# A second norm that carries its weights by rows, and weight parts at two places modulo 256 bytes

## The chip, the cores and the metric

One core of one Trainium2 chip. The metric is the device time of one execution in microseconds (us), the median of several. The engines are TensorE (PE; its weight loads are shown apart as PEld), VectorE (DVE), ScalarE (ACT), GpSimd (POOL) and SyncE (SP), which issues most of the DMAs. TensorE's products land in PSUM, which has eight banks of 128 x 512 float32; everything else that the engines work on lies in SBUF.

## The reference

One layer of an encoder, for 512 rows of 1024 features in float32. What matters here is the second half:

```python
def layer(x):
    h = rmsnorm(x, g_pre_mix)
    q, k, v, g, u, sv, a_ret, a_sgu = split(h @ w_in)          # 1024 x 7168
    merged = sigmoid(a_ret) * retention(q, k, v, g) @ w_ret_o + sigmoid(a_sgu) * sgu(u, sv) @ w_sgu_o
    x1 = x + rmsnorm(merged @ w_out, g_post_mix)
    h2 = rmsnorm(x1, g_pre_ffn)
    hid = conv3(h2 @ w_up)                                     # 1024 x 5632, three taps along the rows, and a bias
    a, b = split(hid)
    return x1 + rmsnorm((gelu(a) * b) @ w_down, g_post_ffn)    # 2816 x 1024

def rmsnorm(x, g):
    return x * rsqrt(mean(x * x) + 1e-6) * g
```

## The kernel before

Each float32 operand of a product is split into a high part, which ScalarE copies (line 79 in `copy`), and a low part, which VectorE gets by subtraction (line 86 in `split`). A product is then three: high by high, high by low and low by high (`mm3`, lines 217 to 219). Of `w_up`, the weights are the stationary operand and the activations the moving one, so the result has features by partitions and rows along the free dimension. `w_down` and `w_out` go the other way round.

Many products come in couples of seven instead of eight (Strassen's scheme in Winograd's form): class `Pair`, whose products all stand on line 670. For these the weights are added in seven forms (`w_form`: B11, B21, T1, T2, T3, T4, B22; T2 and T4 on GpSimd, lines 170 and 172) and the activations in four sums S1 to S4 (`x_forms`). A product of a couple takes 256 of the 512 rows at a time ("in halves"); `T0` and `T1` are the two halves.

The stages, in the order of time: q and k (to 50 us); the retention part with v, the two halves of the SGU's second input and the gate g (to 216 us); `u` in couples (to 260 us); the gates `a_ret` and `a_sgu` in couples, each beside whole blocks of `w_ret_o` or `w_sgu_o` with 512 columns (to 426 us); `w_out` with the two norms (to 487 us); `w_up` (to 712 us); `w_down` (to 825 us); the last norm's rest.

The part around the change, in the kernel's words:

- `norms(t, acc)` does the two norms of one row block of 128 rows: the mean square on ScalarE (`mean_square`), the root on GpSimd (`row_scale`, whose result is called `qr`), `z` and the sum x1 on VectorE, then x1 times the scale of the second norm, called `xn` (line 871).
- `turn(t, zs)` lets TensorE transpose `xn` (line 882). ScalarE copies each block of 128 features from PSUM with its weight of `g_pre_ffn` as the scale into `h2h[k]` (line 886), VectorE makes `h2l[k]` of it (line 889). A weight stands by partition here, since features lie along the partitions.
- `early(e, q)` runs the first four blocks of `w_up` by halves of the rows, so that TensorE can begin with the rows whose norms are done.
- `f_block` runs one further block of `w_up`: 8 feature blocks by 3, in halves where `two` is set and over 512 columns otherwise. Blocks 4 to 7 (tiles 2 and 3) and the whole blocks of the gates take 512 columns.
- `h2_forms(k)`, called after tiles 0 and 1, adds `h2h` and `h2l` of two feature blocks on GpSimd (line 981, the sum is called `h`) and makes S1 to S4 of it (lines 300 to 303 and 79, 86). The couples of `w_up` (tiles 4 to 19) need them.
- `conv`, `gated` and `down_forms` turn the results of `w_up` into what `w_down` takes.

Tiles named `blk` are 512 columns wide and lie in a ring of 76; a weight part is a `slot` of 1088 columns, of which it uses 1024 from column `at` on. As built, every `blk` and every slot begins 64 bytes past a multiple of 256, so `at` (in columns of 4 bytes) sets a weight part's place modulo 256 bytes: 0 leaves it at 64, 16 puts it at 128, 32 at 192 and 48 at 0.

The order of the instructions on each engine is written by a scheduler that reads the program; the DMA queues keep that order too.

Of the kernel before, what the change touches and what calls it, by code (L numbers as in the profile page):

```python
# [10 lines left out]
F32 = mybir.dt.float32  # L11
# [29 lines left out]
PRE, FFNG, LNG, LNB = 0, 8, 16, 24  # L41
CW, CB = 32, 32 + 3 * 2 * NF
# [5 lines left out]
def tile_block(ctx: ExitStack, tc, xT, x, wall, par, cs, wsp, bsp, gpost, gffn, out):  # L48
# [77 lines left out]
    def halved(e):  # L126

        return e < EARLY or e >= 2 * COUPLES[0][0]

    def w_block(i):  # L130
# [26 lines left out]
    def w_form(form, i):  # L157
# [15 lines left out]
        w = slot("wf", 16)  # L173
        split(w[:, :S], w[:, S:], w_raw[form])
        return w[:, :S], w[:, S:]

    def w_down(form, i):
# [15 lines left out]
        hi, lo = slot("dh", 48, w), slot("dl", 48, w)  # L193
# [8 lines left out]

    def w_get(look=LOOK):
# [5 lines left out]
        while w_pos[1] < len(units) and (w_pos[1] <= i or n + w_size(units[w_pos[1]]) <= max(room, 9 if look == LOOK else 0)):  # L209
            u = units[w_pos[1]]  # L210
            w_ready[w_pos[1]] = w_unit(u)
            w_pos[1] += 1
            n += w_size(u)
# [8 lines left out]
    part = const("part", [P, NPAR + 8])[:, :NPAR]  # L222
# [418 lines left out]
    def f_block(ah, al, n, between=None, two=False):  # L641
# [3 lines left out]
        f = (T0, T1) if two else (slice(0, S),)  # L645
        for i in range(n * len(f)):
            if between and i == n * len(f) // 2:
                between()
            k, t = i % n, f[i // n]
            c = slice(k * P, (k + 1) * P)  # L650
            mm3(o[:, t], wh[:, c], wl[:, c], ah[k][:, t], al[k][:, t], k == 0, k == n - 1)
        return o

    class Pair:
# [3 lines left out]
        def __init__(self, func, alloc, a=None, scale=None):  # L658
            self.func, self.t, self.scale = func, [alloc(), alloc()], scale
            self.h, self.l, self.forms = a or (xh, xl, forms)  # L660
# [15 lines left out]
        def x(self, first, t):  # L676
            return lambda k: (self.h[first + k][:, t], self.l[first + k][:, t])
# [46 lines left out]
    for j in range(KD // 2):  # L724
        p = Pair(AF.Gelu_apprx_tanh, lambda: blk(n="u"), None, rbc)
# [40 lines left out]
    def gated_pair(ah, al, late=None):  # L766
        p = Pair(AF.Sigmoid, lambda: tmp("sig"), None, rbc)
# [77 lines left out]
    for k in range(KD):  # L845
        h2h.append(blk(F32R, "h2h"))
        h2l.append(blk(F32R, "h2l"))

    def norms(t, acc):
# [19 lines left out]
        for n in range(2):  # L869
            z = tmp("xn")  # L870
            v.tensor_scalar(
# [384 lines left out]
```

## Time and profile before

| | |
|---|---|
| median of three runs | 837.9 us (836.99 to 840.36) |
| the profiled execution | 835.91 us |
| its span, first to last instruction | 834.1 us |
| granted TensorE clock, mean | 0.993 |
| instructions | 14181 |
| TensorE products | 5632, busy 815.7 us |
| DMA | 93.31 MB, mean 112 GB/s |

The profile is of one execution. Its rows name an engine, a line of the kernel, an operation and its tiles (out<-in, buffer numbers left out), the shape, the count, and what ended the idle time before it. A product's end is modelled, and its recorded time (0.28 us for 256 columns, 0.39 us for 512) overlaps that of the next: how fast products follow each other is read from their starts or from their number in a stretch.

### The profile page before, as it was taken

To read this page: it belongs to the slowest core of one execution; us is meant where nothing else is said; L and a number is where in the kernel's file an instruction comes from. 1 tells how busy PE (TensorE), PEld (TensorE's weight loads), DVE (VectorE), ACT (ScalarE), POOL (GpSimd) and SP (SyncE) were. 2 spreads that over 40 slices of the span, in tenths; PEclk is the share of its full clock that TensorE was granted. 3 is DMA by queue.
4 is the path that set the end of the run, shared out by engine and by line. 5 is a ranking of instruction groups with operands and counts; after the bars stand their busy time and mean duration, and the time that the engine had idled before them with its cause. 6 is when DMAs were issued, how large, how long until landed. Compare 5 with 4: busy or idle time off the path is not lost.

```text
span 834.1 us, 14181 instructions
## 1 busy us (share of the span) xinstructions
PE 815.7 (98%) x5632; PEld 753.4 (90%) x5632; DVE 665.1 (80%) x1100; ACT 429.8 (52%) x729; POOL 110.4 (13%) x110
## 2 busy tenths in 40 slices
PE   9999999999999999999999999899999999999995
PEld 7888888888899999999988898799999999999995
DVE  7489888877897776867664769779899899997956
ACT  6635446545664533444444564456566565654531
POOL 0010000112221111132211225110211100000001
PEclk9999999999999999999999999999999999999998
DMA  8733222213233333323457120333333341243334
GB/s 290 244 114 106 74 74 77 75 51 102 86 104 103 102 102 101 102 76 111 140 157 301 60 68 26 102 101 102 102 103 101 101 153 51 77 127 108 120 127 152
DMA packets 29219, 93.31 MB, mean 112 GB/s; under 512 B 3360, under 2 KB 4000, under 8 KB 29152
## 3 DMA queue, kind: packets, MB, share of 16 engines
q1 hardware_dynamic: 26928, 86.85, 32.4%
q0 software_dynamic: 1360, 4.46, 1.6%
q10 hardware_dynamic: 864, 1.09, 0.4%
q8 instruction: 44, 0.72, 0.3%
q14 instruction: 23, 0.19, 0.1%
HBM read 88.19 MB, written 4.19 MB: 111 GB/s over the span
## 4 chain that ended last, share of the span: by engine, by line
PE 77%; DVE 15%; issue 3%; DMA 2%; ACT 1%; POOL 1%; DVEq 0%; POOLq 0%; ACTq 0%; SPq 0%
PE ps L670 18%; PE ps L217 10%; PE ps L218 10%; PE ps L219 10%; PE ps L1024 7%; PE ps L480 5%; PE ps L479 5%; PE ps L481 5%; DVE wf L86 2%; DVE wl L86 2%; DVE cv L931 2%; PE ps L820 2%; PE ps L819 2%; PE ps L818 2%; DVE cv L935 2%
## 5 line engine op out<-in xcount | busy, mean ns | idle before, releaser
L86 DVE TENSOR_TENSOR wl<-raw,wh 128x1024 fp32r<-128x1024 f32 (+1 forms) x93 | 110.7, 1199 | 49.3 <-PE ps L670 23.5
L79 ACT ACTIVATE wf<-raw 128x512 fp32r<-128x512 f32 x140 | 85.0, 627 | 100.8 <-PE ps L218 35.6
L86 DVE TENSOR_TENSOR wf<-raw,wf 128x512 fp32r<-128x512 f32 x140 | 106.4, 775 | 26.6 <-ACT wf L79 26.0
L670 PE MATMUL ps<-sh,wf 128*128 128x256 f32 x640 | 121.7, 280 | 2.2 <-ACT sh L79 1.7
L217 PE MATMUL ps<-h2h,wh 128*128 128x256 f32 (+1 forms) x416 | 118.7, 287 | 0.0
L219 PE MATMUL ps<-h2h,wl 128*128 128x256 f32 (+1 forms) x416 | 118.6, 286 | 0.0
L218 PE MATMUL ps<-h2l,wh 128*128 128x256 f32 (+1 forms) x416 | 118.6, 286 | 0.0
L79 ACT ACTIVATE wh<-raw 128x1024 fp32r<-128x1024 f32 (+2 forms) x95 | 93.2, 990 | 35.3 <-DMA raw<-wall 14.7
L670 PEld LDWEIGHTS ps<-sh,wf 128*128 128x128 f32 x640 | 102.0, 189 | 3.4 <-ACT sh L79 1.9
L670 PE MATMUL ps<-sl,wf 128*128 128x256 f32 x320 | 89.6, 280 | 1.5 <-DVE sl L86 1.5
L217 PEld LDWEIGHTS ps<-h2h,wh 128*128 128x128 f32 x416 | 78.3, 189 | 1.5 <-ACT h2h L886 0.3
L218 PEld LDWEIGHTS ps<-h2l,wh 128*128 128x128 f32 x416 | 78.3, 188 | 1.3
L219 PEld LDWEIGHTS ps<-h2h,wl 128*128 128x128 f32 x416 | 78.3, 188 | 1.2
L479 PE MATMUL ps<-wh,xh 128*128 128x512 f32 x192 | 75.0, 391 | 0.0
L480 PE MATMUL ps<-wl,xh 128*128 128x512 f32 x192 | 74.9, 390 | 0.0
L481 PE MATMUL ps<-wh,xl 128*128 128x512 f32 x192 | 74.8, 390 | 0.0
L170 POOL TENSOR_TENSOR raw<-raw,raw 128x512 f32<-128x512 f32 x20 | 34.4, 1718 | 218.5 <-DVE raw L168 184.4
L670 PEld LDWEIGHTS ps<-sl,wf 128*128 128x128 f32 x320 | 61.1, 191 | 2.0 <-DVE sl L86 1.7
L1024 PE MATMUL ps<-dl,fh 128*128 128x256 f32 x216 | 59.9, 278 | 1.5 <-DVE dl L86 1.5
L1024 PE MATMUL ps<-dh,fh 128*128 128x256 f32 x216 | 60.0, 278 | 1.2 <-DVE e L1058 1.0
L1024 PE MATMUL ps<-dh,fl 128*128 128x256 f32 x216 | 59.8, 277 | 0.0
L670 PE MATMUL ps<-xh,wf 128*128 128x256 f32 x288 | 54.5, 281 | 0.0
(303 smaller groups left out, 2051.5 us busy)
## 6 DMA issues: line engine op xcount, KB each, us to landing
raw<-wall SPq DMA_DIRECT2D x145, 512.0 KB, 3.6
x<-x SPq DMA_DIRECT2D x24, 256.0 KB, 6.1
xT<-xT SPq DMA_DIRECT2D x8, 256.0 KB, 5.5
x<-x POOLq DMA_DIRECT2D x8, 256.0 KB, 2.3
xT<-xT POOLq DMA_DIRECT2D x4, 256.0 KB, 3.9
out<-zg SPq DMA_DIRECT2D x4, 256.0 KB, 2.2
out<-zs ACTq DMA_DIRECT2D x3, 256.0 KB, 3.7
cs<-cs SPq DMA_DIRECT2D x2, 256.0 KB, 4.2
```

Source lines behind the costliest of these rows:

```text
L79: nc.scalar.activation(out=o, in_=i, func=AF.Copy)
L86: nc.vector.tensor_sub(lo, src, as32(hi))
L170: nc.gpsimd.tensor_tensor(out=w_raw["T2"], in0=w_raw["T1"], in1=w_raw["B22"], op=ALU.add)
L217: nc.tensor.matmul(o, ah, bh, start=start, stop=False)
L218: nc.tensor.matmul(o, ah, bl, start=False, stop=False)
L219: nc.tensor.matmul(o, al, bh, start=False, stop=stop)
L479: nc.tensor.matmul(acc[t], xh[k][:, c], wh[:, f], start=k == 0, stop=False)
L480: nc.tensor.matmul(acc[t], xh[k][:, c], wl[:, f], start=False, stop=False)
L481: nc.tensor.matmul(acc[t], xl[k][:, c], wh[:, f], start=False, stop=k == KD - 1)
L670: nc.tensor.matmul(o, w_[:, c], a_, start=first and k == n == 0, stop=k == 3 and n == 2, skip_group_check=True,)
L818: nc.tensor.matmul(o, ah, bh, start=k == 0, stop=False)
L1024: nc.tensor.matmul(o, a_[:, c], w_[:, f], start=j == t == i == 0, stop=j == DP - 1 and i == 2 and n not in (M2, M3, M4), skip_group_check= ...
```

## The change

1. The second norm's weights come by rows: `g_pre_ffn` is loaded over all partitions (`gpr`, two more DMAs from GpSimd) and multiplied in where `xn` is made. The copies behind the transposes need no scale any more.
2. `h2` lies in other tiles. One tile of 512 columns holds two feature blocks of two row blocks (256 rows) each, so a copy behind the transposes takes 2 x 128 columns. Besides the high part (`h2h`) ScalarE copies the unsplit value (`h2r`).
3. The sums S1 to S4 are made from `h2r`, 512 columns at a time and in place, after tiles 0 and 1 (`h2_sums`). GpSimd's additions are gone. After each the next unit of weights is made too (`w_next`).
4. All blocks of `w_up` run in halves (`up_block`); tiles 2 and 3 had 512 columns.
5. Products in halves get their weight parts at two places modulo 256 bytes. For the couples and `w_up` the high part is now at 0 and the low part at 128 (both were at 128), beside activations at 64. For `w_down`, where weights are the moving operand, the high part is at 128 and the low part at 0 (both were at 0), beside activations at 64.

```diff
-    def halved(e):
-        return e < EARLY or e >= 2 * COUPLES[0][0]
...
     def w_block(i):
...
-            at = 48 if i >= DOWN0 else 16 if i >= UP0 and halved(i - UP0) else 0
-            hi, lo = slot("wh", at), slot("wl", at)
+            hi, lo = (slot("wh", 16), slot("wl", 48)) if i >= DOWN0 else (
+                (slot("wh", 48), slot("wl", 16)) if i >= UP0 else (slot("wh"), slot("wl"))
+            )
...
     def w_form(form, i):
...
-        w = slot("wf", 16)
-        split(w[:, :S], w[:, S:], w_raw[form])
-        return w[:, :S], w[:, S:]
+        w = slot("wf", 0, 1088)
+        hi, lo = w[:, S + 48 : 2 * S + 48], w[:, 16 : S + 16]
+        split(hi, lo, w_raw[form])
+        return hi, lo
...
     def w_down(form, i):
...
-        hi, lo = slot("dh", 48, w), slot("dl", 48, w)
+        hi, lo = slot("dh", 16, w), slot("dl", 48, w)
...
-    gpm = bcast(gpost, "gpm")
-    h2h, h2l = [], []
-    h2forms = {n: [] for n in ("S1", "S2", "S3", "S4")}
+    gpm, gpf = bcast(gpost, "gpm"), bcast(gpre, "gpr")
+    h2h, h2l, h2r = ([[blk(dt, n) for _ in range(4)] for _ in range(2)]
+                     for dt, n in ((F32R, "h2h"), (F32R, "h2l"), (F32, "h2r")))
...
-            v.tensor_scalar(
-                out=z, in0=xt[n], scalar1=sc, scalar2=None, op0=ALU.mult
+            v.scalar_tensor_tensor(
+                out=z, in0=xt[n], scalar=sc, in1=gpf[n], op0=ALU.mult, op1=ALU.mult
             )
...
     def turn(t, zs):
-        c = slice(t * P, (t + 1) * P)
+        g, c = t // 2, slice((t % 2) * P, (t % 2 + 1) * P)
...
-            for f in range(4):
-                k = 4 * n + f
-                pf = p[:, f * P : (f + 1) * P]
-                nc.scalar.activation(
-                    out=h2h[k][:, c], in_=pf, func=AF.Copy, scale=col(FFNG + k)
-                )
-                v.scalar_tensor_tensor(
-                    out=h2l[k][:, c], in0=pf, scalar=col(FFNG + k), in1=as32(h2h[k][:, c]),
-                    op0=ALU.mult, op1=ALU.subtract,
-                )
+            for i in range(2):
+                hi, lo, raw = (h[g][2 * n + i].rearrange(two, i=2)[:, :, c] for h in (h2h, h2l, h2r))
+                pf = p[:, 2 * i * P : 2 * (i + 1) * P].rearrange(two, i=2)
+                copy(hi, pf)
+                copy(raw, pf)
+                v.tensor_sub(lo, pf, as32(hi))
+
+    def h2_parts(n, i, src):
+        h_, l_ = blk(F32R, "sh"), blk(F32R, "sl")
+        split(h_, l_, src)
+        for j in range(2):
+            f = slice(j * 256, (j + 1) * 256)
+            h2forms[n][2 * i + j] = h_[:, f], l_[:, f]
+
+    def h2_sums(i):
+        a0, b0, a1, b1 = h2r[0][i], h2r[0][i + 2], h2r[1][i], h2r[1][i + 2]
+        v.tensor_sub(b1, a1, b1)
+        v.tensor_sub(a1, a0, a1)
+        v.tensor_sub(a0, b1, a0)
+        v.tensor_add(b0, b0, a0)
+        for n, t in zip(("S1", "S2", "S3", "S4"), (b1, a0, a1, b0)):
+            h2_parts(n, i, t)
+
+    def up_block(between=None):
+        w, o = w_get(), ps()
+        h2_block(w, o, T0)
+        if between:
+            between()
+        h2_block(w, o, T1)
+        return o
...
-    def h2_forms(k):
-        h2 = halves("h2")
-        for i in range(2):
-            nc.gpsimd.tensor_tensor(out=h2[i], in0=as32(h2h[k + 4 * i]), in1=as32(h2l[k + 4 * i]), op=ALU.add)
-        x_forms(k, *h2, h2forms)
...
-                o.append(early_o[e] if e < EARLY else f_block(h2h, h2l, KD, None, halved(e)))
+                o.append(early_o[e] if e < EARLY else up_block())
+            if i < 2:
+                h2_sums(i)
+                w_next()
             tile_done(i, o)
-            for k in {0: (0, 1), 1: (2, 3)}.get(i, ()):
-                h2_forms(k)
```

How the order moves. VectorE, from the last low part of `h2` on, before (`cv` are the taps of tiles 0 and 1, `wl` low parts of weights, `xs` and `h` the sums):

```order
L889 SCALAR_TENSOR_TENSOR h2l_4402<-ps_5000,part,h2h_4401 128x128
L86 TENSOR_TENSOR wl_4959<-raw_4956,wh_4958 128x1024
L931 SCALAR_TENSOR_TENSOR cv_5109<-ps_4855,part,cv_5109 128x511
L86 TENSOR_TENSOR wl_5202<-raw_5199,wh_5201 128x1024
L935 SCALAR_TENSOR_TENSOR cv_5109<-ps_4855,part,cv_5109 128x511
L931 SCALAR_TENSOR_TENSOR cv_5113<-ps_4906,part,cv_5113 128x511
L86 TENSOR_TENSOR wl_5208<-raw_5205,wh_5207 128x1024
L935 SCALAR_TENSOR_TENSOR cv_5113<-ps_4906,part,cv_5113 128x511
L168 TENSOR_TENSOR raw_5252<-raw_5217 128x512
L944 TENSOR_TENSOR gp_5118<-cv_5109,cv_5113 128x512
L931 SCALAR_TENSOR_TENSOR cv_5154<-ps_4931,part,cv_5154 128x511
L300 TENSOR_TENSOR xs_5124<-h_881_5120,h_882_5121 128x256
```

The same place after:

```order
L889 TENSOR_TENSOR h2l_4397<-ps_4998,h2h_4389 128x2x128
L908 TENSOR_TENSOR h2r_4405<-h2r_4403,h2r_4405 128x512
L889 TENSOR_TENSOR h2l_4396<-ps_4987,h2h_4388 128x2x128
L889 TENSOR_TENSOR h2l_4398<-ps_4998,h2h_4390 128x2x128
L909 TENSOR_TENSOR h2r_4403<-h2r_4399,h2r_4403 128x512
L86 TENSOR_TENSOR sl_5110<-h2r_4405,sh_5109 128x512
L910 TENSOR_TENSOR h2r_4399<-h2r_4405,h2r_4399 128x512
L86 TENSOR_TENSOR wl_4959<-raw_4956,wh_4958 128x1024
L911 TENSOR_TENSOR h2r_4401<-h2r_4401,h2r_4399 128x512
L86 TENSOR_TENSOR sl_5114<-h2r_4399,sh_5113 128x512
L86 TENSOR_TENSOR wl_5128<-raw_5125,wh_5127 128x1024
```

The first sum stood eleven places behind the last low part of `h2`; now it stands ahead of it.

GpSimd at the same time, before (`raw` are the weight sums T2 and T4):

```order
L837 TENSOR_TENSOR qr_4848<-qs_4847,nhalf 128x1
L981 TENSOR_TENSOR h_881_5120<-h2h_4387,h2l_4388 128x512
L981 TENSOR_TENSOR h_882_5121<-h2h_4395,h2l_4396 128x512
L170 TENSOR_TENSOR raw_5252<-raw_5252,raw_5218 128x512
L981 TENSOR_TENSOR h_888_5137<-h2h_4389,h2l_4390 128x512
L981 TENSOR_TENSOR h_889_5138<-h2h_4397,h2l_4398 128x512
L981 TENSOR_TENSOR h_898_5165<-h2h_4391,h2l_4392 128x512
L981 TENSOR_TENSOR h_899_5166<-h2h_4399,h2l_4400 128x512
L172 TENSOR_TENSOR raw_5252<-raw_5252,raw_5218 128x512
```

And after:

```order
L865 DMA x_30_4413<-x_861_4825 128x512
L865 DMA x_31_4414<-x_862_4826 128x512
L839 TENSOR_TENSOR qr_4852<-qs_4851,nhalf 128x1
L167 TENSOR_TENSOR raw_5244<-raw_5244,raw_5186 128x512
L169 TENSOR_TENSOR raw_5244<-raw_5244,raw_5186 128x512
```

The eight additions are gone, and the weight sums follow the norms directly. What TensorE does in the couples stays as it was.

More of the change, by code (lines that the diff above doesn't have):

```diff
@@ L47, in tile_block @@
 @with_exitstack
-def tile_block(ctx: ExitStack, tc, xT, x, wall, par, cs, wsp, bsp, gpost, gffn, out):
+def tile_block(ctx: ExitStack, tc, xT, x, wall, par, cs, wsp, bsp, gpost, gpre, gffn, out):
     nc = tc.nc
@@ L900, in early @@
             early_o.append(ps())
-        wh, wl = early_w[e]
-        f = slice(q * 256, (q + 1) * 256)
-        for k in range(KD):
-            c = slice(k * P, (k + 1) * P)
-            mm3(early_o[e][:, f], wh[:, c], wl[:, c], h2h[k][:, f], h2l[k][:, f], k == 0, k == KD - 1)
+        h2_block(early_w[e], early_o[e], (T0, T1)[q])
     dn_ = Down(mh, ml, KD, RES_OUT)
@@ L1242 @@
         "gpost": i["g_post_mix"],
+        "gpre": i["g_pre_ffn"],
         "gffn": i["g_post_ffn"],
```

60 lines of the change are left out of this document (35 added, 25 removed).

## The prediction

> **What bounds the kernel.** I read the page's busy shares first, then the busy time by stretch, then who waited for whom on TensorE, then the two places that these pointed at in order of time. The profiled execution took 835.9 us with a span of 834.1 us, 2.0 us under the median of the three runs (837.9 us).
>
> ```profile
> PE 815.7 (98%) x5632; PEld 753.4 (90%) x5632; DVE 665.1 (80%) x1100; ACT 429.8 (52%) x729; POOL 110.4 (13%) x110
> ```
>
> TensorE is busy for 98% of the span, so only two things can move the time: a stretch where TensorE stands still, and the pace of its products while it runs. The next rows give, for seven stretches, their length, the busy time (and instructions) of PE, PEld, DVE, ACT and POOL, the granted clock, DMA share and GB/s.
>
> ```profile
> 490.00:498.90 8.90, 8.90 (x78) 8.90 (x77) 7.31 (x10) 6.49 (x9) 0.53 (x1) 1.00 0.40 120
> 499.50:519.50 20.00, 20.00 (x90) 16.56 (x89) 20.00 (x31) 10.25 (x17) 10.35 (x8) 1.00 0.08 27
> 491.00:524.50 33.50, 33.50 (x198) 29.74 (x197) 32.29 (x45) 18.70 (x27) 11.52 (x8) 1.00 0.16 49
> 524.50:533.00 8.50, 4.87 (x24) 4.27 (x23) 8.50 (x17) 4.99 (x9) 0.00 (x0) 0.80 0.53 181
> 560.00:640.00 80.00, 80.00 (x708) 80.00 (x707) 72.69 (x113) 49.30 (x85) 10.12 (x7) 1.00 0.32 101
> 646.50:711.50 65.00, 65.00 (x576) 65.00 (x575) 60.17 (x96) 39.71 (x64) 4.03 (x3) 1.00 0.31 98
> 712.40:729.40 17.00, 17.00 (x146) 17.00 (x146) 16.64 (x31) 10.01 (x16) 0.00 (x0) 1.00 0.30 93
> ```
>
> Two things are to be seen. First, in 524.5 to 533.0 us TensorE works 4.87 of 8.50 us at a granted clock of 0.80, while VectorE is never idle: it worked 32.29 of the 33.50 us before that too. VectorE is what is late there. Second, the pace. A product of 256 columns is recorded as 0.28 us long, so a stretch counts about 0.28 us worth of products too many, and the pace is (length + 0.28) / count: 113.4 ns in 560 to 640, 113.3 ns in 646.5 to 711.5, but 118.3 ns in 712.4 to 729.4 and 117.7 ns in 490 to 498.9, all at clock 1.00. Products of 512 columns (recorded 0.39 us) go at 20.39 / 90 = 226.6 ns. So the same kind of product has a fast rhythm and a slow one, 4.5 ns apart.
>
> ```profile
> PE ps L670 <- ACT sh L79: 1.7, 1, 1.7
> PE ps L1024 <- DVE dl L86: 1.5, 1, 1.5
> PE ps L670 <- DVE sl L86: 1.5, 1, 1.5
> ```
>
> TensorE's three longest waits: two are for `sh` and `sl`, the two parts of a sum of h2, in the first couple of w_up's products (L670); the third is for a weight part of the down product, at 729 us.
>
> ```profile
> 524.58 0.28 PE L670 MATMUL ps<-sh,wf 128*128 128x256 f32 x1
> 526.60 0.38 PE L670 MATMUL ps<-sh,wf 128*128 128x256 f32 x1 [1.74 <-ACT sh L79]
> 528.47 0.39 PE L670 MATMUL ps<-sl,wf 128*128 128x256 f32 x1 [1.49 <-DVE sl L86]
> 528.69 0.28 PE L670 MATMUL ps<-sh,wf 128*128 128x256 f32 x1
> 529.38 0.44 PE L670 MATMUL ps<-sh,wf 128*128 128x256 f32 x1 [0.41 <-ACT c L79]
> ```
>
> **The sums of h2, and the stall.** Why they are late, on VectorE and on GpSimd:
>
> ```profile
> 487.55 3.15 DVE L889 SCALAR_TENSOR_TENSOR h2l<-ps,part,h2h 128x128 fp32r<-128x128 f32 x8 [3.74 <-ACT h2h L886]
> ...
> 503.90 1.77 DVE L86 TENSOR_TENSOR sl<-xs,sh 128x512 fp32r<-128x512 f32 x1
> 505.59 1.51 DVE L303 TENSOR_TENSOR h<-h,xs 128x256 f32<-128x256 f32 x1
> 507.02 0.73 DVE L935 SCALAR_TENSOR_TENSOR cv<-ps,part,cv 128x511 f32<-128x511 f32 x1
> 507.68 1.21 DVE L86 TENSOR_TENSOR wl<-raw,wh 128x1024 fp32r<-128x1024 f32 x1
> 508.82 0.68 DVE L86 TENSOR_TENSOR sl<-h,sh 128x512 fp32r<-128x512 f32 x1
> ```
>
> ```profile
> 500.77 6.04 POOL L981 TENSOR_TENSOR h<-h2h,h2l 128x512 f32<-128x512 f32 x4
> ```
>
> While GpSimd adds h2h and h2l back together, an `sl` takes 1.77 us instead of 0.68. The change drops these eight adds. Its sums start from h2r, which ScalarE has copied, stand in VectorE's queue right behind the last `h2l` and are eight operations of 512 columns (0.68 us each, as `sl`) where there were sixteen of 256. By the new order VectorE has, from the last `h2l` (490.7 us) to the last part of S4: 8 sums and 8 `sl` of 0.68, 3 `wl` of 1.21, 8 `cv` of 0.73 and one product of 0.68: 10.9 + 3.6 + 5.8 + 0.7 = 21.0 us, so 511.7 us. TensorE asks for the first sum not before 523 us: a margin of 11 us. The stall goes. In the stretch from 524.5 to 533.0 us stand 24 products; at 113.4 ns they take 24 x 0.1134 = 2.72 us of 8.50 + 0.28. Worth 8.78 - 2.72 = **6.06 us**, the products at half the clock behind the stall included. What is late next is the weight part of tile 3's last block, a `cv` and a `wl` (0.73 + 1.21 us) behind S4, at 513.6 us. TensorE needs it after the early blocks (498.9 us) and three blocks of 48 products, 3 x 5.44 us: 515.2 us. That is the thinnest margin; I price it at 0, with up to 1 us for the range.
>
> **The copies.** Each row block now takes 4 copies to h2h and 4 to h2r where it took 8.
>
> ```profile
> L79 ACT ACTIVATE c<-ps 128x256 f32<-128x256 f32 x32 | 12.1, 378 | 22.9 <-PE ps L670 22.8
> L886 ACT ACTIVATE h2h<-ps,part 128x128 fp32r<-128x128 f32 x32 | 11.1, 364 | 10.6 <-PE ps L882 6.2 <-DVE h2l L889 4.1
> ```
>
> A copy of 256 columns from PSUM costs 378 ns against 364 ns for 128, so ScalarE's 8 per row block stay at 3.0 us. For the last row block TensorE waits for them directly. The copy that holds feature block 2 is fifth in ScalarE's queue in both kernels: ready after 5 x 0.378 = 1.9 us now, 5 x 0.364 = 1.8 us before; bounds -0.3 us (half as many low parts on VectorE) and +0.6 us (an h2r copy ahead of each pair); I take +0.2 us, nearest the two rows.
>
> **Norm's weights by rows.** The scaling of 2 x 512 columns becomes an operation with a third operand.
>
> ```profile
> L861 DVE SCALAR_TENSOR_TENSOR z<-ps,qr,gpm 128x512 f32<-128x512 f32 x8 | 6.0, 747 | 1.6 <-POOL qr L837 1.6
> ...
> L871 DVE TENSOR_SCALAR xn<-x,qr 128x512 f32<-128x512 f32 x8 | 3.5, 484 | 1.5 <-POOL qr L837 1.5
> ```
>
> ```profile
> 480.84 0.48 DVE L871 TENSOR_SCALAR xn<-x,qr 128x512 f32<-128x512 f32 x1 [0.30 <-POOL qr L837]
> ```
>
> ```profile
> 486.52 1.03 PE L882 MATMUL ps<-ident,xn 128*128 128x128 f32 x8
> ```
>
> It costs 2 x (747 - 484) = 0.5 us per row block. In the last block xn starts at 480.84 us and TensorE turns it at 486.52: 4.6 us of cover, so 0. Without that cover it would cost 0.5 us once. The two new loads of g_pre_ffn stand in GpSimd's queue behind those of g_post_mix:
>
> ```profile
> 431.52 1.11 POOL L797 DMA_DIRECT2D gpm<-gpost  x2
> 449.23 0.57 POOL L837 TENSOR_TENSOR qr<-qs,nhalf 128x1 f32<-128x1 f32 x1 [16.60 <-DVE qs L834]
> ```
>
> 1.1 us more of issue inside 16.60 us of idle: 0. Tiles 2 and 3 go from 96 products of 512 columns to 192 of 256: 2 x 113.4 = 226.8 against 226.6 ns, so 0 in the fast rhythm and 192 x 4.5 = 0.9 us in the slow one.
>
> **The places modulo 256 bytes.** In units of 64 bytes, the moving operands of these products sat at 1 and the weights loaded beside them at 2 (down product: 0 and 1), so the load was always one unit ahead. Now the high part's load is one unit behind (0 against 1; down product: 1 against 2) and the low part's one ahead: of three products two have the new distance. What the trace shows of distance: the first and the last of 32 products of the retention part, where both stand at 1 (distance none), and of 48 products in the gates' stage, one unit ahead.
>
> ```profile
> 86.26 0.28 PE L218 MATMUL ps<-vl,sm 128*128 128x256 f32 x1
> ...
> 89.98 0.28 PE L219 MATMUL ps<-vh,sm 128*128 128x256 f32 x1
> ```
>
> ```profile
> 366.43 0.28 PE L670 MATMUL ps<-xh,wf 128*128 128x256 f32 x1
> ...
> 371.97 0.28 PE L670 MATMUL ps<-sh,wf 128*128 128x256 f32 x1
> ```
>
> 3.72 / 31 = 120.0 ns with no distance; 5.54 / 47 = 117.9 ns in the gates' stage and 113.3 in 646.5 to 711.5, both one unit ahead. So distance matters, and one unit ahead has two rhythms that last: the slow one begins at 712.4 us, with the first down product, and ends with the wait at 729. One unit behind is not in this trace. Bounds: 113.3 ns (the pace at which 256 and 512 columns cost the same per column) and 120.0 ns. I take 113.4: it is 64 bytes from the moving operand, as the fast row is, not on it, as the 120 ns row is; and a rhythm that needs every load at one distance has nothing to lock to when the distance changes twice in three products. Then what was slow becomes fast: 672 products of the gates' stage (8 couples of 7 x 12), 192 of the early blocks (4 x 48), 36 ahead of the stall: 900 x 4.5 = **4.0 us**. The 144 slow ones at 712 us give nothing: VectorE worked 16.64 of 17.00 us there and TensorE then waits for `dl`; they would wait longer.
>
> The skill speaks against this part. The Trainium skill, "SBUF — State Buffer", section "SBUF: two separate sides", has it that inside the engine side only the port pair shared by VectorE and GpSimd makes anyone wait, and that TensorE waits for no one at SBUF. By it the place of the weights would count for nothing and the sum would lack the 4.0 us (the time of rival (a) below). The 120.0 ns row against 113.3 speaks against that, though the two come from different stages.
>
> **Sum**, on the profiled time: 835.9 - 6.06 - 4.0 + 0.2 = 826.0 us. Runs centre up to 2.0 us higher; I say 827.
>
> **Rivals.**
> (a) The rhythm belongs to the stage, not to the place: the gates stay slow, the couples fast. 835.9 - 6.06 + 0.2 = 830.0 us. For it: one distance has both rhythms. Against: 120.0 ns.
> (b) The slow rhythm stays. It rules at 490 us, and what comes after the stall is fast: the stall may be what ends it, as at 729 us. With the stall gone it would run on: 192 products of tiles 2 and 3, and from 533 us on 107 / 0.1134 = 940 (if something ends it at 640) to 179 / 0.1134 = 1,580 more (up to 712): x 4.5 ns, 5.1 to 8.0 us given back on the 830.0 of (a), 835.1 to 838.0 us, no change.
> (c) Slower: one unit behind is worse, 120.0 ns. Two in three of the products in halves have it, some 2,620 (of 1,680 in couples, 1,344 in w_up's blocks and 947 in the down product): 2,620 x 6.6 = 17.3 us on the 826, 843 us. It decides from 117.1 ns on: 2,620 x 3.7 = 9.7 us eats both gains.
> (d) Part of the stall returns, at tile 3's last weight part or as a longer wait at 729 us: half of 6.06, 829 us.
>
> **How the numbers follow.** Forecast (824 to 829) 0.50; (a) 0.13; (b) 0.14; (c) 0.15; (d) 0.08. 0.5% is 4.2 us of 837.9, about what a measurement here tells from no change. Faster: forecast, (a) and most of (d), 0.69; same: (b) and a mild (c), 0.16; slower: 0.15. The range 823 to 840 leaves out the worst of (c) and little below: with the down side bounded by TensorE's fast pace, 0.15 at most.
>
> **What would show it.** Right: no wait of TensorE for `sh` or `sl` in the first couple and a granted clock of 1.00 there; `sl` at 0.68 us throughout; 113.4 ns per product in the gates' stage (5.3 us where 48 took 5.5) and in the couples. Wrong: 118 ns in the couples is (b), 117 ns or more wherever weights are in two places is (c), a wait for `wl` near 515 us is (d).

## The result, and the profile after

The changed kernel took 832.8 us, the median of 8 runs (830.76 to 833.83), beside 839.17 us for the kernel before (8 runs, 836.99 to 843.15): ratio 0.9921, 95% interval 0.9904 to 0.9939. That is 0.8% faster, and the interval lies clear of no change: 6.4 us where 10.9 were forecast. It is inside the range of 823 to 840 us, but outside the 824 to 829 us that had a chance of one half. The profiled execution took 833.83 us with a span of 832.1 us; the sum had said 826.0 us for it.

The busy row of the page, TensorE's longest waits, and two of the prediction's stretches, all of the changed kernel (PE, PEld, DVE, ACT, POOL, granted clock, DMA share, GB/s):

```profile
PE 820.3 (99%) x5728; PEld 762.0 (92%) x5728; DVE 660.1 (79%) x1076; ACT 428.8 (52%) x729; POOL 100.2 (12%) x104
```

```profile
PE ps L265 <- DVE raw L260: 1.0, 1, 1.0
PE ps L605 <- DVE o L615: 0.3, 1, 0.3
PE ps L1050 <- DVE yy L1085: 0.2, 1, 0.2
PE ps L219 <- DVE h2l L889: 0.2, 1, 0.2
```

```profile
491.00:524.50 33.50, 33.50 (x298) 33.50 (x297) 32.09 (x47) 21.20 (x33) 2.60 (x2) 1.00 0.25 80
524.50:533.00 8.50, 8.50 (x78) 8.50 (x77) 5.91 (x10) 3.39 (x6) 2.12 (x1) 1.00 0.40 124
```

The stall is gone: no wait for `sh`, `sl` or `dl` is left, 78 products stand in 524.5 to 533.0 us instead of 24, and the clock is 1.00. VectorE worked as much as before ahead of it (32.09 of 33.50 us), but the sums come first and nothing slows them: GpSimd has no instruction from 487 to 510 us, and all eight `sl` take 0.68 to 0.69 us. The last four of them begin and end with these rows:

```profile
502.85 0.69 DVE L86 TENSOR_TENSOR sl<-h2r,sh 128x512 fp32r<-128x512 f32 x1
...
507.83 0.68 DVE L86 TENSOR_TENSOR sl<-h2r,sh 128x512 fp32r<-128x512 f32 x1
```

What did not come as forecast is the pace. Here TensorE alone is read over five stretches (length, busy time and products, clock, DMA share, GB/s). The kernel before:

```profile
226.00:256.00 30.00, 30.00 (x267) 1.00 0.30 92
535.00:635.00 100.00, 100.00 (x884) 1.00 0.33 105
646.00:703.00 57.00, 57.00 (x505) 1.00 0.36 112
734.00:764.00 30.00, 30.00 (x267) 1.00 0.37 116
780.00:815.00 35.00, 35.00 (x311) 1.00 0.37 121
```

The changed kernel:

```profile
226.00:256.00 30.00, 30.00 (x255) 1.00 0.32 103
535.00:635.00 100.00, 100.00 (x885) 1.00 0.34 105
646.00:703.00 57.00, 57.00 (x482) 1.00 0.33 102
734.00:764.00 30.00, 30.00 (x257) 1.00 0.39 122
780.00:815.00 35.00, 35.00 (x300) 1.00 0.33 106
```

By (length + 0.28) / count, before was fast in all five: 113.4 ns, 113.4, 113.4, 113.4, 113.4. After is 118.7 ns in u, 113.3 in w_up up to the sixth couple, 118.8 ns behind 640 us and 117.8 and 117.6 in the two halves of the down product. So the changed kernel has slow rhythms too, and now they stand where the kernel before was fast. The gates became fast: the first and the last product of one of their groups of 48 in the changed kernel give 5.33 / 47 = 113.4 ns.

```profile
367.35 0.28 PE L672 MATMUL ps<-xh,wf 128*128 128x256 f32 x1
...
372.68 0.28 PE L672 MATMUL ps<-sh,wf 128*128 128x256 f32 x1
```

By stages (us), each from the start of its first product to that of the next stage. The gates are counted from their first product of 512 columns, so 48 products of their first couple stand in u; w_up is counted from behind the last transposes, so the first halves of its early blocks stand in w_out. The rows from the third on are of the experiments below:

| profiled execution | u | gates | w_out | w_up | w_down and rest | span |
|---|---|---|---|---|---|---|
| before | 43.94 | 165.57 | 61.32 | 224.87 | 121.67 | 834.1 |
| after | 46.00 | 163.03 | 62.10 | 221.53 | 122.33 | 832.1 |
| after, once more | 46.00 | 163.03 | 62.06 | 218.22 | 123.16 | 829.1 |
| norm and sums alone | 45.58 | 165.57 | 62.00 | 226.27 | 121.99 | 838.1 |
| places alone | 45.75 | 163.03 | 61.30 | 228.15 | 122.66 | 838.0 |
| before, one wide product | 43.97 | 165.57 | 61.33 | 231.23 | 119.88 | 838.9 |
| both parts one behind | 45.58 | 165.15 | 62.05 | 226.26 | 122.24 | 838.6 |
| both parts two units off | 45.91 | 167.19 | 62.14 | 227.97 | 123.45 | 843.4 |
| both parts at the same place | 46.40 | 166.81 | 62.23 | 230.51 | 123.78 | 846.5 |
| places exchanged | 43.96 | 163.26 | 61.74 | 218.25 | 122.89 | 826.9 |

From before to after that is +2.06, -2.54, +0.78, -3.34 and +0.66 us, and 0.33 us ahead of u: -2.0 us between these two profiles. The medians lie 6.4 us apart. The likely reason is that the profile of before had the fast rhythm in more stages than most of its runs: its 835.9 us stands at the lower end of the 835.8 to 844.8 us that the runs of the same kernel took beside the experiments.

### The profile page after: what moved, and what is told of

It is laid out like the page before. It is cut to its first block, busy times and chain, and to the rows that moved or that the text cites. A ratio compares the mean times of both kernels' runs of the same rounds, so it can differ in the third digit from the quotient of the medians.

```text
span 832.1 us, 14355 instructions
## 1 busy us (share of the span) xinstructions
PE 820.3 (99%) x5728; PEld 762.0 (92%) x5728; DVE 660.1 (79%) x1076; ACT 428.8 (52%) x729; POOL 100.2 (12%) x104
## 5 line engine op out<-in xcount | busy, mean ns | idle before, releaser
L219 PE MATMUL ps<-h2l,wh 128*128 128x256 f32 x448 | 124.6, 279 | 0.2 <-DVE h2l L889 0.2
L218 PE MATMUL ps<-h2h,wh 128*128 128x256 f32 x448 | 123.7, 278 | 0.0
L220 PE MATMUL ps<-h2h,wl 128*128 128x256 f32 x448 | 123.7, 277 | 0.0
L672 PE MATMUL ps<-sh,wf 128*128 128x256 f32 x640 | 120.1, 277 | 0.1
L219 PEld LDWEIGHTS ps<-h2l,wh 128*128 128x128 f32 x448 | 83.9, 187 | 0.7 <-DVE h2l L889 0.7
L218 PEld LDWEIGHTS ps<-h2h,wh 128*128 128x128 f32 x448 | 83.8, 188 | 0.3 <-ACT h2h L79 0.3
L220 PEld LDWEIGHTS ps<-h2h,wl 128*128 128x128 f32 x448 | 83.9, 188 | 0.0
```

The lines of the kernel that those rows point to most:

```text
L218: nc.tensor.matmul(o, ah, bh, start=start, stop=False)
L219: nc.tensor.matmul(o, ah, bl, start=False, stop=False)
L220: nc.tensor.matmul(o, al, bh, start=False, stop=stop)
L672: nc.tensor.matmul(o, w_[:, c], a_, start=first and k == n == 0, stop=k == 3 and n == 2, skip_group_check=True,)
```

## The experiments

Two questions were open: which half of the change brought the gain, and what decides which rhythm a run of products falls into.

**Norm, tiles and sums alone.** The changed kernel with the places of before:

```diff
-            hi, lo = (slot("wh", 16), slot("wl", 48)) if i >= DOWN0 else (
-                (slot("wh", 48), slot("wl", 16)) if i >= UP0 else (slot("wh"), slot("wl"))
-            )
+            at = 48 if i >= DOWN0 else 16 if i >= UP0 else 0
+            hi, lo = slot("wh", at), slot("wl", at)
...
-        w = slot("wf", 0, 1088)
-        hi, lo = w[:, S + 48 : 2 * S + 48], w[:, 16 : S + 16]
+        w = slot("wf", 16)
...
-        hi, lo = slot("dh", 16, w), slot("dl", 48, w)
+        hi, lo = slot("dh", 48, w), slot("dl", 48, w)
```

> The changed kernel with the places of before (high and low parts both one unit ahead of the other operand); norm, tiles and sums as changed. In every theory the stall at 524 us is gone and the gates go at 117.8 ns again (+3.0 us on 832.8), u at 113.3 (-1.9). Theory A (the rhythm has a memory; which one a run of products falls into is set by how it begins, and with these places it begins slow behind products of 512 columns and fast behind a wait of TensorE): w_up begins slow at about 478 us and has no wait before about 640 us, so some 1,440 of its products go at 117.8 ns (+6.5); behind that wait they go fast (-3.4), and the down product mostly fast (-4.2, of which waits for VectorE take back 3.5): 833 to 837 us in all, no faster than before. Theory B (the place alone sets the rhythm in each stage, without memory): w_up's couples go at 113.3 ns throughout, as before from 533 us on, 827 to 831 us.

Measured: 832.46 us, the median of 10 runs (829.86 to 840.26), ratio 0.9949 (0.9912 to 0.9986). The runs lie apart: six from 829.9 to 832.6 us, one at 837.2, three from 839.9 to 840.3. The profile is of one of the last three. Its couples, on TensorE:

```profile
535.00:635.00 100.00, 100.00 (x852) 1.00 0.34 100
646.00:703.00 57.00, 57.00 (x486) 1.00 0.33 104
```

100.28 / 852 = 117.7 ns and 57.28 / 486 = 117.9: from 491 to 715 us all is slow, 1,900 products, although the stall is gone. This is the prediction's rival (b), at 839.9 us. Theory A holds for this execution in w_up, but not for u, where a run that began behind a wait was slow. Theory B falls. The wait at 640 us did not happen here (TensorE came late enough), so nothing ended the rhythm. That the six shorter runs were fast in w_up is inferred from their times alone. All ten ran on one chip, so the two groups are no difference between chips.

**The places alone.** The kernel before with the new places; its blocks of 512 columns kept theirs. The edit is the change's three hunks on places.

> The kernel before with the new places alone (blocks of 512 columns keep theirs); norm, tiles and sums as before, so the stall stays. Gates at 113.5 ns (-3.0 us on 839.2), u at 118.9 (+1.9). Theory A (memory; with the new places a run of products begins fast behind products of 512 columns and slow behind a wait): behind the stall at 533 us all couples go at 118.9 ns (some 1,550 products x 5.6 = +8.7) and the down product at 117.8 (+3.5, less 3.5 of waits for VectorE): 844 to 849 us, slower than before. Theory B (place and stage, no memory): couples fast to about 640 us as in the changed kernel, slow behind: 840 to 843 us.

Measured: 843.1 us (10 runs, 837.92 to 845.24), ratio 1.0036 (1.0004 to 1.0067): no gain, a small loss. So the gain comes from the norm, the tiles and the sums; the median of that half alone (832.46 us) is about that of the whole change, and that the places add to it is not shown by these times. What they change is seen in the stages. The gates take 163.03 us as in the changed kernel, 2.54 less than before, but u takes 1.81 us more and w_up 3.28 us more. Behind the stall, which theory A had as the start of the slow rhythm, the couples were fast; behind the wait at 645 us they were slow, as this profile's rows on TensorE show:

```profile
535.00:635.00 100.00, 100.00 (x885) 1.00 0.33 105
646.00:703.00 57.00, 57.00 (x481) 1.00 0.35 110
```

So a wait starts a run of products either way, and A's rule on waits falls. The paces are those that theory B had named for this kernel, and its 840 to 843 us is close; but B cannot explain the run before.

**A wide product as a new start.** One more product, of 512 columns, in the changed kernel behind the wait at 640 us, and its mirror in the kernel before:

```diff
-        def product(self, b, act, first, w=None):
+        def product(self, b, act, first, w=None, wide=None):
             wh, wl = w or w_get()
+            if wide is not None:
+                nc.tensor.matmul(self.b[b], wh[:, :P], wide, start=True, stop=True, skip_group_check=True)
...
-            p.part1()
+            p.part1(h2h[0][0] if i == 16 else None)
```

> The changed kernel with one more product: of 512 columns, into a bank that the next product overwrites, ahead of the first product of the couple of tiles 16 and 17 (about 644 us, some 4 us behind the wait of 0.39 us at which the products turned slow). It costs 0.23 us by itself. Theory A (memory; a product of 512 columns lets the rhythm begin anew, and with the new places fast): 113.3 ns from 644 us to the end of w_up instead of 118.9, -3.1 us, 829.9 us, and down to 826 if the down product begins fast from there. Theory C (the slow pace from 640 us on is of the stage, of what the other engines do to SBUF then): 118.9 ns stays, 833.0 us.

> The mirror of it: the kernel before with the same one product of 512 columns at the same place in the code, where its products are fast. Theory A (with the old places a run begins slow behind products of 512 columns): 117.8 ns from about 650 us to 712 us instead of 113.3, some 550 products, +2.5 us on TensorE there; the wait at 729 us for VectorE shrinks by up to its 1.78 us, so 839.5 to 842 us in all. Theory C (the pace is of the stage): 113.3 ns stays, 839.4 us.

Neither of the two told what it was made for. In the changed kernel (831.3 us, 6 runs, ratio 0.9918, 0.989 to 0.9945) the products were fast behind the wait already, ahead of the added one. In the kernel before (840.19 us, 10 runs, ratio 1.0024, 0.9997 to 1.0052) they were slow already from the stall on:

```profile
535.00:635.00 100.00, 100.00 (x851) 1.00 0.32 100
```

117.8 ns where the first profile of the same instructions up to there had 113.4. That is the more useful reading: behind the stall the kernel before may go on fast or slow, and its w_up then takes 224.87 or 231.23 us (3.7 of these 6.4 us lie ahead of the added product, where the instructions are the same). What the prediction took for a rule ("a wait ends the slow rhythm") was one toss of a coin.

**The changed kernel once more.**

> The changed kernel once more, unchanged, to see how far its rhythm differs from run to run. Theory D (the rhythm of a run of products is left to chance where it begins behind a wait of TensorE, and is set by the places where it begins behind products of 512 columns or where the order of high and low parts breaks): gates again 113.5 ns and 490 to 640 us again 113.3 ns, while u (118.9 ns in the first profile) and the stretch behind the wait at 640 us (118.9 there) may come out either way; times in two groups some 2.5 us apart, 831 and 833.5 us. Theory E (no chance: the same program gives the same rhythm): the same pace in every stage, times within 0.3 us of one another but for drift.

Measured: 831.27 us (6 runs: 830.76 to 831.48 four times, 832.97 and 833.05), ratio 0.9927 (0.9908 to 0.9945). The two groups are there. The span of this profile is 829.1 us; the wait at 639 us was followed by fast products:

```profile
646.00:703.00 57.00, 57.00 (x505) 1.00 0.32 101
```

57.28 / 505 = 113.4 ns, against 118.8 in the first. w_up takes 218.22 us, 3.3 less; 0.8 us of it is lost again in the down product, where TensorE now waits 0.6 us for `dl`. Theory E falls. What is the same in both profiles, to 0.01 us, is u (46.00, slow) and the gates (163.03, fast).

**Wide products where the rhythm is slow.** Four of them: in u at 234 us, ahead of the couple of tiles 16 and 17, and one near the start of each half of the down product (the edit as above, and in `products` ahead of the loop over `t`).

> The changed kernel with four products of 512 columns whose results are overwritten: in u (ahead of its third couple, 234.5 us, in a stretch that was slow in both profiles of the new places), ahead of the couple of tiles 16 and 17 (644 us), and one near the beginning of each half of the down product (712 and 771 us, slow in each profile of the new places). Each costs 0.23 us. Theory D (behind a product of 512 columns the places set the rhythm, and the new ones give the fast one): 113.3 ns from 234.5 us to 263 us (250 products x 5.6 = -1.4), behind 644 us always, and in both halves of the down product; in the down product VectorE then takes most of it back as waits near 729 and 771 us (up to 3.5 us), so 828.5 to 831 us. Theory F (one such product does nothing, the gates are fast for another reason): 118.9 ns in u and 117.8 in the down product as before, 833.5 us.

Measured: 830.68 us (4 runs, 830.41 to 834.77), ratio 0.9926 (0.99 to 0.9952). In u, on TensorE from 236 us on:

```profile
236.00:256.00 20.00, 20.00 (x179) 1.00 0.31 99
```

20.28 / 179 = 113.3 ns where the two profiles of the changed kernel have 118.6 (171 products). So behind a product of 512 columns the changed places do begin fast. The same is seen behind the wait at 639 us in a later profile, the first of the two attempts below, which has such a product there: its products go slowly from the wait to the added product on line 668, 4.16 us / 35 = 118.9 ns,

```profile
638.59 0.28 PE L674 MATMUL ps<-sl,wf 128*128 128x256 f32 x1
...
642.75 0.40 PE L668 MATMUL ps<-h2h,wf 128*128 128x512 f32 x1
```

and fast behind it, 59.78 / 528 = 113.2 ns:

```profile
643.50:703.00 59.50, 59.50 (x528) 1.00 0.34 104
```

In the down product of the kernel with four wide products nothing changed: 257 products in 734 to 764 us, 117.8 ns. Theory D holds for the couples, theory F for the down product.

**Distance by itself.** Three kernels with both weight parts at one place, so that every load has the same distance. The edit is that of the first experiment with other numbers: columns 48 (couples, w_up) and 16 (down product) for one unit behind; 32 and 32 for two units; 0 and 0 for the same place.

> The changed kernel with both weight parts one unit behind the other operand (couples and w_up: both at 0 beside 64; down product: both at 128 beside 64), so the distance no longer changes from product to product. Read in the gates, where the start is the same in every run. Theory G (what frees the gates of the slow rhythm is that the distance changes): 117 to 118 ns in the gates, +3 us on 832.8. Theory H (what frees them is that most loads are one unit behind): 113.3 to 113.6 ns there, 832 us.

> The changed kernel with both weight parts two units (128 bytes) from the other operand, as far as places modulo 256 bytes allow: couples and w_up at 192 beside 64, down product 192 beside 64. Theory I (a load disturbs the products the less the farther it is): 113.3 ns in the gates, in u and in the down product in every run, no slow rhythm at all; u -1.9 us, 640 us on -3.3, down product 4.2 less of which VectorE takes 3.5 back: 827 us. Theory D without that (each distance has both rhythms): 113.3 or 117 to 120 ns in the gates, both paces elsewhere, 830 to 838 us.

> The changed kernel with both weight parts at the place of the other operand (64 beside 64, down product too), the distance that the retention part has and where its products took 120.0 ns. If the place alone makes that price: 120.0 ns in u, in the gates and in w_up and the down product, whatever stands ahead; from 832.8 us that is 672 x 6.6 (gates) + 345 x 1.1 (u) + 1,300 x 6.7 (490 to 640 us) + 590 x 1.1 + 930 x 2.2 = 4.4 + 0.4 + 8.7 + 0.6 + 2.0, so 849 us. If the retention part's pace was of its stage, the pace lies between 113 and 118 ns and the time below 840 us.

| weight part, seen from the moving operand | median (runs) | ratio | gates, group of 48 | 535 to 635 us |
|---|---|---|---|---|
| both one unit ahead (before) | | | 117.8 ns | 113.4 or 117.8 ns |
| high one behind, low one ahead (after) | 832.8 (8) | 0.9921 | 113.4 | 113.3 |
| both one behind | 839.65 (10) | 1.0017 (1.0004 to 1.0031) | 117.8 | 117.7 |
| both two off | 844.99 (4) | 1.0084 (1.0063 to 1.0105) | 120.1 | 118.7 |
| both at the same place | 848.48 (2) | 1.0105 (1.0051 to 1.0158) | 119.8 | 120.0 |

The rows behind it, each the stretch from 535 to 635 us on TensorE; first one unit behind:

```profile
535.00:635.00 100.00, 100.00 (x852) 1.00 0.33 101
```

then two units off:

```profile
535.00:635.00 100.00, 100.00 (x845) 1.00 0.31 94
```

and the same place:

```profile
535.00:635.00 100.00, 100.00 (x836) 1.00 0.30 92
```

Nothing but addresses differs between these three kernels and the changed one: the instructions stand in the same order on every engine. That it is the distance that counts, and not the place of the weights by itself, follows from the down product, where the weights are the moving operand: there both parts at 0 have been fast and both at 128 go at 117.8 ns (257 products in 734 to 764 us), while in the couples both at 128 have been fast and both at 0 go at 117.7. The same place costs 119.8 to 120.2 ns in u, gates, w_up and down product and came out at 848.5 us where 849 was expected. One unit behind has no fast rhythm anywhere in its profile, and its ten runs lie within 1.0 us. Two units off is no remedy (theory I falls, and the 830 to 838 us of theory D for it were missed too). In these profiles only the distance of before, and a distance that changes, have the fast rhythm; the gates, whose groups begin behind products of 512 columns, were slow with the first and fast with the second in every profile (theory G, not H).

**The places exchanged.** High part ahead, low part behind (down product likewise):

```diff
-            hi, lo = (slot("wh", 16), slot("wl", 48)) if i >= DOWN0 else (
-                (slot("wh", 48), slot("wl", 16)) if i >= UP0 else (slot("wh"), slot("wl"))
+            hi, lo = (slot("wh", 48), slot("wl", 16)) if i >= DOWN0 else (
+                (slot("wh", 16), slot("wl", 48)) if i >= UP0 else (slot("wh"), slot("wl"))
...
-        hi, lo = w[:, S + 48 : 2 * S + 48], w[:, 16 : S + 16]
+        lo, hi = w[:, S + 48 : 2 * S + 48], w[:, 16 : S + 16]
...
-        hi, lo = slot("dh", 16, w), slot("dl", 48, w)
+        hi, lo = slot("dh", 48, w), slot("dl", 16, w)
```

> The changed kernel with the two places exchanged: couples and w_up have the high part at 128 and the low part at 0 beside 64, the down product the high part at 0 and the low part at 128 beside 64. Of three loads two are then one unit ahead and one behind, where the change has two behind and one ahead. Theory G (what frees the gates is that the distance changes within three products): 113.3 to 114 ns in the gates, 829 to 834 us. Theory M (it takes two loads behind and one ahead): 117 to 119 ns in the gates, +3 us there.

Measured: 829.02 us (2 runs, 828.7 and 829.33), ratio 0.9873 (0.9821 to 0.9925), and fast in u, in both parts of w_up and in the gates (113.8 ns), behind the same waits:

```profile
226.00:256.00 30.00, 30.00 (x267) 1.00 0.31 91
535.00:635.00 100.00, 100.00 (x884) 1.00 0.34 106
646.00:703.00 57.00, 57.00 (x505) 1.00 0.29 92
734.00:764.00 30.00, 30.00 (x257) 1.00 0.38 117
```

Theory G; M falls. The down product stays at 117.8 ns.

**Two attempts at a better kernel.** The first has the changed couples, the down product's places of before and two wide products (in u and at tiles 16 and 17); the second the exchanged couples, the down product's places of before, and no added product.

> The changed kernel with the down product's weight parts back at the places of before (both at 0 beside 64), and with two products of 512 columns whose results are overwritten: one in u behind its last wait (about 227 us) and one ahead of the couple of tiles 16 and 17. Theory K (the slow rhythm of the down product comes from its new places, which have shown no other in 13 starts, while the places of before have shown both): the down product now shows 113.3 ns in one of its stretches at least; u at 113.3 ns from 227 us on (-1.5 us), 641 to 706 us fast in every run; 827 to 829.5 us. Theory L (the down product is slow because of what the other engines do then): 117.8 ns in all its stretches, 830 us.

> The changed kernel with high and low places exchanged in couples and w_up (high at 128, low at 0 beside 64), and the down product's parts back at the places of before (both at 0). If the exchanged places have only the fast rhythm, u, gates and w_up go at 113.3 to 113.6 ns in every run: the times no longer fall into two groups 2.5 us apart, and what spread is left is the down product's, whose places have both rhythms by chance (861 products x 4.5 = 3.9 us, of which VectorE's waits at about 721 and 764 us take back up to 2.5). 826.5 to 829.5 us. If the exchanged places have both rhythms too and the run before this one was lucky, one of u, 487 us or 637 us shows 117 to 119 ns, or times beyond 831 us.

Measured: 829.89 us (6 runs, 828.33 to 832.91), ratio 0.9886 (0.9851 to 0.9922), and 828.21 us (6 runs, 826.38 to 830.99), ratio 0.9888 (0.9853 to 0.9922). In both profiles one of the down product's two stretches is fast, not the same one; the first kernel's 734 to 764 us and the second's 780 to 815 us:

```profile
734.00:764.00 30.00, 30.00 (x267) 1.00 0.35 107
```

```profile
780.00:815.00 35.00, 35.00 (x312) 1.00 0.38 120
```

Theory K holds by the pace, though the first kernel's median lies 0.4 us above its range: 30.28 / 267 = 113.4 ns with the places of before, which no profile with the changed or exchanged places shows in the down product. It is worth little: in the first kernel TensorE then stands still for 1.6 us at 764 us, waiting for VectorE. In the second kernel u takes 43.96, the gates 163.26 and w_up 218.31 us, within 0.1 us of the profile with the places exchanged: fast in every stage with couples, as its expectation had it, and its median lies in the range given, though its runs spread beyond it on both sides. Both medians are lower than the changed kernel's, but the intervals of their ratios overlap with its 0.9904 to 0.9939, and they did not run beside it: that they beat it is likely, by the stages, and not shown by the times.

## Why the prediction was right in its direction and too large

**The stall, -6.06 us: right.** In the second profile of the changed kernel, where nearly all of w_up is fast from 490 us on, w_up took 218.22 us instead of 224.87: -6.65. The sum has for this stage the stall, 96 products of the early blocks' second halves and the 36 ahead of the stall, 6.06 + 132 x 4.5 ns = 6.65. VectorE was free even earlier than reckoned: the last `sl` ended at 508.5 us, forecast 511.7.

**The gates, 672 x 4.5 = 3.0 us: right, mis-sized by 0.5.** 113.4 ns as said, and 2.54 us in the stage. Of the 672 products, 48 stand in u, ahead of the first product of 512 columns; they were fast before and are slow now.

**Copies +0.2, norm by rows 0: the place was wrong.** At the last turn, for which both were reckoned, nothing changed: TensorE's first weight load behind it waits 0.27 us for `h2h`, 0.26 before. But w_out grew by 0.78 us, 0.5 of it in two gaps of TensorE at w_up's first products, which wait for `h2l`. VectorE's queue and TensorE's weight loads there, changed kernel:

```profile
472.67 1.42 DVE L870 SCALAR_TENSOR_TENSOR xn<-x,qr,gpr 128x512 f32<-128x512 f32 x2 [0.74 <-POOL qr L839]
474.00 0.75 DVE L889 TENSOR_TENSOR h2l<-ps,h2h 128x256 fp32r<-128x256 f32 x2
```

```profile
474.48 0.19 PEld L219 LDWEIGHTS ps<-h2l,wh 128*128 128x128 f32 x1 [0.33 <-DVE h2l L889]
475.63 0.19 PEld L219 LDWEIGHTS ps<-h2l,wh 128*128 128x128 f32 x1 [0.38 <-DVE h2l L889]
```

The same two `xn` in the kernel before, and what stands ahead of them:

```profile
473.37 0.35 DVE L889 SCALAR_TENSOR_TENSOR h2l<-ps,part,h2h 128x128 fp32r<-128x128 f32 x1
474.02 0.88 DVE L871 TENSOR_SCALAR xn<-x,qr 128x512 f32<-128x512 f32 x2 [0.30 <-POOL qr L837]
```

They take 1.42 us now instead of 0.88, and stand ahead of the `h2l` of an earlier row block for which TensorE is waiting. The order adds to it: before, five of the eight `h2l` of that row block stood ahead of `xn`, one of them beside GpSimd's root `qr`, for which VectorE then idled 0.30 us; now it idles 0.74 us there, and every `h2l` of the block stands behind `xn`. How much of the two gaps comes from the longer operation and how much from the order was not separated. The prediction had looked at the cover of the last row block only. Its "0.5 us once" without cover is about what the gaps cost, but it is the price of the operation alone, so that the two agree is in part luck.

**The step that failed: "a rhythm that needs every load at one distance has nothing to lock to when the distance changes twice in three products".** It was true in the gates, behind products of 512 columns, and in w_up's couples up to 639 us, which were fast in all six profiles with the changed places. It was false elsewhere: u was slow in every profile of the changed kernel until an added product of 512 columns stood in it; behind the wait at about 639 us three of the six were fast and three slow; the down product was slow throughout. The sum held u, the part behind 640 us and the down product at their fast pace of before and so lacked 2.06, 3.3 and 0.66 us in the profile of the changed kernel. With 1.0 us in w_out (0.78 where the sum had -0.2, since the first halves of the early blocks stayed slow too), 0.46 in the gates and 0.33 ahead of u, these are the 7.8 us between 826.0 and 833.8.

**The base was lucky.** The sum started from a profile in which u, w_up behind the stall and most of the down product were fast. The kernel before with one product added at 654 us shows the other way out, 6.4 us longer in w_up, 3.7 of it ahead of that product. The prediction put 2.0 us between profile and median and took that for chance in the runs; it was probably this.

**The rivals.** By its number (a) is the nearest, 830.0 us and up to 2.0 more, and that is chance: (a) falls, since the gates' pace follows the place, and the time is as it is because u, the end of w_up and w_out took back what the gates gave. (b), the slow rhythm running on without the stall, is real: it is what the norm and sums alone do in part of their runs, at 839.9 us and more where 835.1 to 838.0 was said. With the changed places no profile has it in w_up's couples ahead of 639 us, and none of the 14 runs of the changed kernel took more than 833.83 us, where four in ten took 837.2 or more without them. (c) asked whether one unit behind is worse. It is no 120.0 ns but 117.7 with no fast rhythm, above the 117.1 given as the point of decision; but with two loads in three one behind the pace is 113.3 or 118.9. (Two thirds of its 3,971 products are 2,647 and not 2,620, which would make 0.2 us.) (d) did not come: the wait at 639 us stood in the kernel before as well, at 645 us, with 0.36 us from one product's start to the next. Of the down product it was right that a faster pace brings longer waits for VectorE, as the 1.6 us at 764 us behind a fast stretch show.

**The place of the weights.** The Trainium skill, "SBUF — State Buffer", section "SBUF: two separate sides", has TensorE wait for no one at SBUF. The prediction took it that by this rule the place of the weights would count for nothing. The changed kernel and the three that differ from it in addresses alone show that it counts: 113.3, 117.7, 118.7 and 120.0 ns for the same products. Whether TensorE waits for another engine there or is in its own way, no view shows.

**Where the wait at 639 us comes from.** VectorE's queue in the changed kernel with the weight load that waits for it, and GpSimd's sum of weights beside it:

```profile
637.67 1.66 DVE L86 TENSOR_TENSOR wf<-raw,wf 128x512 fp32r<-128x512 f32 x1
639.26 0.41 DVE L700 TENSOR_TENSOR c<-ps,c 128x256 f32<-128x256 f32 x1
...
639.72 0.19 PEld L672 LDWEIGHTS ps<-sh,wf 128*128 128x128 f32 x1 [0.31 <-DVE c L700]
```

```profile
637.14 1.64 POOL L167 TENSOR_TENSOR raw<-raw,raw 128x512 f32<-128x512 f32 x1 [16.79 <-DVE raw L165]
```

A `wf` that takes 0.68 us at 639.59 took 1.66 us just before, while GpSimd adds; the subtraction behind it reads its PSUM bank late, and TensorE's next product into that bank waits 0.31 us. It is the case of the eight additions that the change removed, in another place. Moving that sum off GpSimd was not tried.

**What stays open.** Why a run that begins behind a wait falls into one rhythm or the other, why the changed places begin slow in u in every profile and by chance at 639 us, and why the down product's changed places are never fast though their distances change in the same order. The runs show that addresses and the way a run begins decide; no view shows the mechanism.

## What to carry to other kernels

When TensorE is busy for 98% of the span, count products in stretches of equal kind: a pace that is 4 to 6% off in one stage is a term of its own, and here it was as large as the stall. Before summing against one profiled execution, ask which of its stages could have come out otherwise in the next run, by the spread of the runs and by a second profile. And when a stage gets an operation of 0.25 us more, look at what stands behind it in that queue at every turn, not only at the last.

## What the runs showed of the hardware that was not expected

- A product of 256 columns follows the one before it after 113.3 ns at best; where the loaded weights and the moving operand stand at the same place modulo 256 bytes it takes 120.0, at 128 bytes 118.7 (120.1 in the gates), 64 bytes behind 117.7, 64 bytes ahead either 113.4 or 117.8, and with the high part behind and the low part ahead either 113.3 or 118.9, each for hundreds of products on end at a granted clock of 1.00.
- The rhythm has a memory: in the kernel with the old places and the new sums 1,900 products in a row stayed slow. In the profiles a long run changed its pace at a wait, at a product of 512 columns or where the order of the operands changed. With high parts one ahead and low parts one behind, u, the gates and w_up's couples were fast in both profiles.
- Times of one kernel therefore spread: 829.9 to 840.3 us with one distance that has both rhythms, 839.35 to 840.35 us with one that has only the slow one.
